# A decoder layer on one core: opening bias table written from 128 partitions, and splits, evacuations and side copies re-ordered

## The chip, the core and the metric

The kernel runs on one core of a Trainium2 chip. The metric is the device time of one execution in microseconds (us); lower is better. Names of engines: PE is TensorE (PEld its weight loads), DVE VectorE, ACT ScalarE, POOL GpSimd, SP the engine that only issues DMAs here.

## The reference

One post-norm decoder layer is applied to a prompt of 512 tokens and to 8 short sequences of 8 new tokens (576 token columns in all), width 1024, in float32:

```python
h = x @ w_in                                   # u | v | q | k | v_att | gate_A | gate_B
y_A = gelu(u) * (tril(W_s[g]) @ LN(gelu(v)) + b_s[g])
y_B = sliding-window attention, 16 heads over 4 key/value heads, window 128,
      scores + rel_bias[bucket(distance)], softmax with one learned sink per head
m   = (sigmoid(gate_A) * (y_A @ w_pa) + sigmoid(gate_B) * (y_B @ w_pb)) @ w_o
x   = LN(alpha * x + m);  x = LN(alpha * x + (silu(x @ w_gate) * (x @ w_up)) @ w_down)
```

What matters here is the bias: for the prompt, a block of 128 queries by 128 keys of head h needs `rel_bias[bucket((q - k) mod 128), h]`, a matrix that is one row of 128 numbers turned by one place per query.

## The kernel before

**Splits.** Every float32 product is made of three products of fp32r pieces: `split` (lines 114 to 116) makes `hi` on ACT and `lo = raw - hi` on DVE. All weights lie in one DRAM tensor `wall`, cut into units of 128 x 1024 in the order of use. `fetch` (L125) loads units into three `raw` buffers from SP's queue, so unit i+3 can be loaded only when DVE has made `lo` of unit i. `convert(n)` splits the units up to n and fetches two ahead; `unit` hands out the next one.

**The opening** is in `projections_and_attention`. Units 0 and 1 hold the first key tile (`ps0_0`) and the first query tile (`ps0_1`), worked through in eight steps k, each with its slice of x. After k = 1 `bias_products(0)` multiplies a selector matrix by the bias table into `bias_0` (16 heads x 512), DVE copies it into `bout` (L437), and `bias_tables` writes it to DRAM (`circ`, 1 MB: 16 heads, each of their rows repeated 128 times, L444), to read it back skewed as `Bsel` (two loads, L448). After k = 4 `bias_products(1)` does the rest for the sample. Then come `evac_k` (tiles `kt`, L469 and L472) and `evac_q` (tiles `qs` and `Z`, L484 to L495), the copies `XS` (L740, L741), the query tile `psq` of unit 2, and `values` (unit 3 and 4 into five `psav` banks, with the first two `attention_scores`, `sc`, between them).

**Attention** runs over 16 blocks (g, n). In each, `attention_turn` transposes the block's probabilities (`pT`), splits them (`pt`), and for n > 0 masks them on POOL by four selects (L600: `pc`, `pt`); `attention_values` multiplies (`po`) and adds the halves into `yB` (L616); the scores of the block two ahead follow; and a fill, `column_tile`, computes 128 more columns of `h` from one weight unit and evacuates them at once. `sample_keys`, called in block (3, 0), loads the cached keys and values and puts the new keys in by 16 small POOL copies (`kc`, L633). `gmlp` later needs `wd`, eight tiny DMAs (L841) and a select on POOL (L843).

A scheduler of the framework orders the instructions of each engine by its own costs, within the dependencies, except where `issue_after` or `manual_schedule` pins them. Each engine then runs its list in order; all DMAs named here stand in SP's queue.

Of the kernel before, what the change touches and what calls it, by code (L numbers as in the profile page):

```python
# [11 lines left out]
F32 = mybir.dt.float32  # L12
F32R = mybir.dt.float32r
I32 = mybir.dt.int32
AF = mybir.ActivationFunctionType
# [15 lines left out]
DS = 8  # L31
W = 128
# [7 lines left out]
NBIAS = W + DS * SK  # L40
# [37 lines left out]
class Builder:  # L78
# [337 lines left out]
    def bias_lookup(self):  # L416

        nc = self.nc
        n1 = NBKT + 1
        self.rb = rb = self.pk.tile([P, H], F32, name="rb")  # L420
        self.bout = []
        self.sel = sel = [self.C([w], F32, f"bsel{w}") for w in (512, NBIAS - 512)]
        nc.gpsimd.memset(rb[:n1], 1.0)
        nc.sync.dma_start(out=rb[:NBKT], in_=self.I["rel_bias"])
        nc.sync.dma_start(out=sel[0][:n1], in_=self.I["bias_sel"][:, :512])

    def bias_products(self, part):
        nc = self.nc
        n1 = NBKT + 1
        sel = self.sel[part]  # L430
        w = sel.shape[1]
        out = self.C([w], F32, f"bout{part}")
        self.bout.append(out)
        for c in range(0, w, 512):
            o = self.bank(f"bias{part}_{c}")[:H, : min(512, w - c)]
            self.mm(o, self.rb[:n1], sel[:n1, c : min(c + 512, w)], True, True)
            nc.vector.tensor_copy(out=out[:H, c : min(c + 512, w)], in_=o)  # L437

    def bias_tables(self):

        nc = self.nc
        cd = self.pd.tile([H, W, W], F32, name="circ")
        out0 = self.bout[0]
        nc.sync.dma_start(out=cd, in_=out0[:H, :W].unsqueeze(1).to_broadcast([H, W, W]))  # L444
        self.Bsel = [self.C([8, P], F32, f"Bsel{i}") for i in range(2)]
        for i in range(2):
            src = bass.AP(cd.tensor, cd.offset + 8 * i * W * W, [[W - 1, P], [W * W, 8], [1, P]])
            nc.sync.dma_start(out=self.Bsel[i][:], in_=src)  # L448

    def sample_bias(self):  # L450
        nc = self.nc
        sd = self.pd.tile([H, DS * SK], F32, name="samp")
        out0, out1 = self.bout
        self.bias_s = self.misc[:, 768:904]
        nc.sync.dma_start(out=sd[:, : 512 - W], in_=out0[:H, W:])
        nc.sync.dma_start(out=sd[:, 512 - W :], in_=out1[:H])
        nc.sync.dma_start(out=self.bias_s, in_=sd.rearrange("h (t j) -> (h t) j", t=DS))

# [17 lines left out]
    def evac_q(self, ps, c):  # L476
        nc = self.nc
        t = self.C([2, NT], F32R, f"qs{c}")
        self.qs[c] = t
        f = lambda a: a.rearrange("p (b c) -> p b c", b=2)  # L480
        for i in range(2):
            s = slice(64 * i, 64 * i + 64)
            o = slice(64 - 64 * i, 128 - 64 * i)
            nc.scalar.activation(out=f(t[s, i]), in_=ps[s, :, :HB], func=AF.Copy, scale=HD ** -0.5)  # L484
            nc.vector.scalar_tensor_tensor(
                out=f(t[o, i]), in0=ps[s, :, :HB], scalar=HD ** -0.5, in1=f(t[s, i]).bitcast(F32),
                op0=ALU.mult, op1=ALU.subtract)
            g, r = c // 2, 2 * (c % 2) + i
            src = ps[s, 1, HB - NS : HB].rearrange("p (a b t) -> p a b t", a=2, b=4)
            for a in range(2):  # L490
                dst = self.Z[64 * a : 64 * a + 64, g].rearrange("p b (r t) -> p b r t", r=4)[:, :, r]
                if a == i:
                    nc.scalar.activation(out=dst, in_=src[:, a], func=AF.Copy, scale=HD ** -0.5)
                else:
                    nc.vector.tensor_scalar_mul(dst, src[:, a], HD ** -0.5)  # L495

    def values(self, between):

        nc = self.nc
        u = [self.unit(4) for _ in range(2)]  # L500
        self.av = [self.C([2, G, 2 * HD], F32R, f"av{i}") for i in range(2)]
        vout = self.SG("vout")
        self.avS = self.misc[:, 512:768]
        for t in range(NB + 1):
            if t in (2, 4):
                between()
            o = self.bank(f"psav{t}")[:, :256]
# [77 lines left out]
    def attention_turn(self, g, n, pr):  # L585

        nc = self.nc
        po = self.bank(f"pT{g}_{n}")
        for r in range(4):
            self.last_turned = nc.tensor.transpose(  # L590
                po[:, P * r : P * r + P], pr[:, r], self.ident[:])
        pt = self.R([2, 512], F32R, f"pt{g}_{n}")
        self.split(pt[:, 0], pt[:, 1], po)
        if n == 0:
            return [(pt, 0)]
        pc = self.R([2, 512], F32R, f"pc{g}_{n}")
        f = lambda a: a.rearrange("p (h q) -> p h q", h=4)
        for out, sign, cmp in ((pc, 1, ALU.is_ge), (pt, -1, ALU.is_gt)):
            for i in range(2):
                nc.gpsimd.affine_select(  # L600
                    out=f(out[:, i]), in_=f(pt[:, i].bitcast(F32)), pattern=[[0, 4], [sign, P]],
                    compare_op=cmp, fill=0.0, base=0, channel_multiplier=-sign)
        return [(pc, n), (pt, n - 1)]
# [16 lines left out]
    def sample_keys(self):  # L620
        nc = self.nc
        f32c = lambda s, n: self.C(s, F32, n)
        kc = [f32c([2, G, SK], f"kc{i}") for i in range(2)]
        vc = [f32c([4, G * HD], f"vc{i}") for i in range(2)]
        for i in range(2):
            nc.sync.dma_start(out=kc[i][:, :, :, :W], in_=self.I["kcT"][:, 2 * i : 2 * i + 2])
            nc.sync.dma_start(out=vc[i][:], in_=self.I["vcT"][:, 4 * i : 4 * i + 4])
        for g in range(G):
            src = self.kraw[64 * (g % 2) : 64 * (g % 2) + 64, g // 2, P:]
            src = src.rearrange("p (a j b t) -> p a j b t", a=2, j=2, b=2)  # L630
# [76 lines left out]
    def projections_and_attention(self):  # L707
# [12 lines left out]
        for k in range(KC):  # L720
# [4 lines left out]
            for c in range(2):  # L725
                wh, wl = (w[:, k % 4, P * c : P * c + P] for w in u)
                for b in range(2):
# [2 lines left out]
                    self.mm(o, wh, xh[:, s], k == 0, False)  # L730
                    self.mm(o, wh, xl[:, s], False, False)
                    self.mm(o, wl, xh[:, s], False, k == KC - 1)
            if k == 1:
                self.bias_products(0)
                self.bias_tables()
            if k == 4:
                self.bias_products(1)
        self.evac_k(tiles[0], 0)
        self.evac_q(tiles[1], 0)
        nc.vector.tensor_copy(out=self.XS[:, :, :NS], in_=self.X[:, :, NP:NT].bitcast(F32))  # L740
        nc.vector.tensor_copy(out=self.XS[:, :, NS:], in_=self.X[:, :, NT + NP :].bitcast(F32))  # L741
        self.run(self.column_tile("q", 1))
        self.yB = []
        blocks = [(g, n) for g in range(G) for n in range(NB)]
        fills = FILLS
# [4 lines left out]
        for i, (g, n) in enumerate(blocks):  # L750
# [3 lines left out]
            if i:  # L754
                with self.tc.issue_after(self.last_turned.ins):
                    self.attention_values(*waiting)
            if i + 2 < len(blocks):
                probs.append(self.attention_scores(*blocks[i + 2]))
                if i + 4 == len(blocks):
                    kc, vc = self.sample_keys()  # L760
            elif i + 1 < len(blocks):
                S = self.sample_scores(kc)
            waiting = g, n, turned
# [2 lines left out]
            if i + 1 == len(blocks):  # L766
                with self.tc.issue_after(self.last_mm.ins):
                    self.attention_values(*waiting)
            self.run(fill)
        self.sample = S, vc  # L770

    def sample_first(self):
# [8 lines left out]
    def column_tile(self, kind, c):  # L781
# [3 lines left out]
        self.fm(ps, u, self.xact, ks=range(7))  # L785
        yield
        self.fm(ps, u, self.xact, ks=range(7, KC))
        if kind == "k":
            self.evac_k(ps, c)
        elif kind == "q":  # L790
# [34 lines left out]
    def gmlp(self):  # L825
# [12 lines left out]
        wd = self.pk.tile([P, 8, NS], F32, name="wd")  # L838
        nc.gpsimd.memset(wd[:NS], 0.0)
        for b in range(DB):  # L840
            nc.sync.dma_start(  # L841
                out=wd[DS * b : DS * b + DS, :, DS * b : DS * b + DS], in_=self.I["wsT"][:DS, :, :DS])
        nc.gpsimd.affine_select(  # L843
            out=wd[:NS], in_=wd[:NS], pattern=[[0, 8], [1, NS]], compare_op=ALU.is_ge, fill=0.0, base=0,
            channel_multiplier=-1)
# [602 lines left out]
```

## Time and profile before

| | before |
|---|---|
| median of 3 runs (lowest to highest) | 900.64 us (899.96 to 900.70) |
| the profiled execution: its time, its span | 901.71 us, 900.0 us |
| PE busy | 880.3 us, 98% of the span |
| DVE, ACT, POOL busy | 632.2, 403.5, 190.9 us |
| DMA | 91.98 MB, mean 102 GB/s |
| chain that ended last | PE 81%, DVE 9%, ACT 4%, DMA 3% |

The page gives busy times over the span. Idle PE time is what can be won, and it is found by the places where PE waits, with the clock that TensorE was granted there. A row of the timeline reads: start, duration, engine, line, operation, output and inputs, count, and in brackets the engine's idle time ahead of it with what ended it.

### The profile page before, as it was taken

The numbers are of one execution on the slowest core, as the hardware profiler recorded it, in microseconds if no ns is written. First come the engines' busy times: TensorE is split into PE (matmuls) and PEld (weight loads), VectorE is DVE, ScalarE is ACT, GpSimd is POOL, SyncE is SP. The second block draws the span as 40 slices with busy tenths as digits, with TensorE's granted clock in tenths as the row PEclk, the third lists the DMA queues.
The fourth block names the chain that finished last, engine by engine and source line by source line (L and its number), as shares of the span: only waits on it lengthen the run. The fifth ranks groups of instructions, "written<-read, shape, count | busy, mean of one in ns | idle before, by whom it ended". The sixth has DMA issues, their size and how long they took to land.

```text
span 900.0 us, 14730 instructions
## 1 busy us (share of the span) xinstructions
PE 880.3 (98%) x5915; PEld 824.0 (92%) x5915; DVE 632.2 (70%) x933; ACT 403.5 (45%) x767; POOL 190.9 (21%) x206
## 2 busy tenths in 40 slices
PE   9799999999999999999999999999999999999996
PEld 7699999997899999999988999999999998888885
DVE  4578978764789878957868777777777779224236
ACT  4456655666355437333442454444444457111110
POOL 2002223332333211233311312222222220000004
PEclk9899999999999999999999999999999999999999
DMA  7731212526223124223570023322233335322202
GB/s 213 211 104 47 71 49 59 169 82 203 87 71 103 60 94 173 87 86 118 188 240 29 1 71 94 94 95 94 94 94 95 94 94 188 90 75 94 71 4 102
DMA packets 32524, 91.98 MB, mean 102 GB/s; under 512 B 3974, under 2 KB 11030, under 8 KB 32424
## 3 DMA queue, kind: packets, MB, share of 16 engines
q1 hardware_dynamic: 32264, 88.86, 30.7%
q10 hardware_dynamic: 192, 2.18, 0.6%
q8 instruction: 46, 0.75, 0.3%
q14 instruction: 22, 0.18, 0.1%
HBM read 86.90 MB, written 6.10 MB: 103 GB/s over the span
## 4 chain that ended last, share of the span: by engine, by line
PE 81%; DVE 9%; ACT 4%; DMA 3%; issue 1%; POOL 1%; SPq 0%; POOLq 0%; ACTq 0%
PE d L296 16%; PE xf L296 14%; PE zf L296 7%; PE acc_v L296 6%; PE pspa L296 6%; PE acc_o L296 6%; PE xg L296 5%; PE yf L296 4%; DMA raw<-in_wall_dram 3%; PE ffn L296 3%; PE zg L296 2%; PE xp L296 2%; ACT work L576 2%; PE psg L296 1%; PE psu L296 1%
## 5 line engine op out<-in xcount | busy, mean ns | idle before, releaser
L116 DVE TENSOR_TENSOR lo<-raw,hi 128x1024 fp32r<-128x1024 f32 (+1 forms) x78 | 90.6, 1169 | 108.0 <-ACT hi L115 107.0
L116 DVE TENSOR_TENSOR glo<-raw,ghi 128x1024 fp32r<-128x1024 f32 (+1 forms) x93 | 100.8, 1087 | 55.2 <-ACT ghi L115 55.2
L115 ACT CAST hi<-raw 128x1024 fp32r<-128x1024 f32 (+1 forms) x78 | 75.6, 983 | 117.8 <-PE d L296 82.6
L296 PE MATMUL d<-hi,h 128*128 128x512 f32 (+1 forms) x440 | 128.0, 368 | 0.0
L115 ACT CAST ghi<-raw 128x1024 fp32r<-128x1024 f32 (+1 forms) x93 | 83.3, 899 | 58.7 <-DVE raw L178 54.1
L296 PEld LDWEIGHTS d<-hi,h 128*128 128x128 f32 x440 | 79.8, 188 | 13.8
L296 PE MATMUL d<-lo,h 128*128 128x512 f32 (+1 forms) x242 | 89.6, 370 | 0.0
L178 POOL TENSOR_TENSOR raw<-raw,t 128x512 f32<-128x512 f32 x31 | 40.7, 1314 | 197.9 <-DVE glo L116 151.4
L178 POOL TENSOR_TENSOR t<-raw,raw 128x512 f32<-128x512 f32 x31 | 43.1, 1389 | 116.3 <-DVE raw L178 116.3
L296 PE MATMUL xf<-x1T,ghi 128*128 128x288 f32 x320 | 65.0, 295 | 0.0
L116 DVE TENSOR_TENSOR glo<-t,ghi 128x1024 fp32r<-128x1024 f32 x31 | 64.5, 2082 | 0.0
L296 PEld LDWEIGHTS d<-lo,h 128*128 128x128 f32 x242 | 45.6, 189 | 7.8
L296 PEld LDWEIGHTS xf<-x1T,ghi 128*128 128x128 f32 x320 | 51.4, 188 | 0.2 <-DVE u L227 0.2
L326 POOL TENSOR_SCALAR lnr<-lnmv 128x1 f32<-128x1 f32 (+1 forms) x15 | 13.6, 904 | 169.2 <-DVE lnmv L344 165.9
L296 PE MATMUL xf<-x1T,glo 128*128 128x288 f32 x160 | 47.1, 294 | 0.0
L296 PE MATMUL acc_o<-hi,m 128*128 128x512 f32 x144 | 46.3, 391 | 0.0
L296 PE MATMUL pspa<-yA,hi 128*128 128x288 f32 x256 | 44.7, 295 | 0.3 <-DVE yA L116 0.3
L296 PE MATMUL psu<-X,hi 128*128 128x288 f32 x256 | 44.1, 294 | 0.0
L576 ACT ACTIVATE work<-work,att 128x128 f32<-128x128 f32 x64 | 25.0, 391 | 37.6 <-DVE att L573 37.6
L296 PE MATMUL acc_v<-hi,X 128*128 128x512 f32 x128 | 41.6, 391 | 0.0
L600 POOL TENSOR_SCALAR_AFFINE_SELECT pc<-pt 128x512 fp32r<-128x512 f32 x24 | 16.1, 672 | 112.7 <-ACT pt L115 108.4
L296 PE MATMUL psq<-X,hi 128*128 128x288 f32 x224 | 38.6, 294 | 0.0
(366 smaller groups left out, 2487.3 us busy)
## 6 DMA issues: line engine op xcount, KB each, us to landing
raw<-in_wall_dram SPq DMA_DIRECT2D x133, 512.0 KB
xr<-in_xT_dram SPq DMA_DIRECT2D x8, 288.0 KB
z<-in_xtok_dram SPq DMA_DIRECT2D x4, 512.0 KB
xraw<-in_xT_dram SPq DMA_DIRECT2D x3, 576.0 KB
out_y_prompt_dram<-z SPq DMA_DIRECT2D x3, 512.0 KB
circ<-bout SPq DMA_DIRECT2D x1, 1024.0 KB
Bsel<-circ SPq DMA_DIRECT2D x2, 512.0 KB
kc<-in_kcT_dram SPq DMA_DIRECT2D x2, 512.0 KB
```

Of the source, the lines that this page charges most:

```text
L115: self.nc.scalar.copy(out=hi, in_=src)
L116: return self.nc.vector.tensor_tensor(out=lo, in0=src, in1=hi.bitcast(F32), op=ALU.subtract)
L178: sub = lambda e, out, x, y: e.tensor_tensor(out=out, in0=x, in1=y, op=ALU.subtract)
L296: self.last_mm = self.nc.tensor.matmul(out, l, r, start=start, stop=stop, **more)
L326: self.nc.gpsimd.tensor_scalar_add(r[:n], mv[:n, 1:2], EPS)
L576: nc.scalar.activation(out=pr[:, r], in_=sel[:, r], func=AF.Exp, bias=nm[:, r : r + 1], accum_out=rs[:, r : r + 1])
L600: nc.gpsimd.affine_select(out=f(out[:, i]), in_=f(pt[:, i].bitcast(F32)), pattern=[[0, 4], [sign, P]], compare_op=cmp, fill=0.0, base=0, c ...
```

## The change

It does five things. The bias row is computed for 128 partitions (each head eight times, by a repeated copy `rb8` made on POOL), repeated four times along the free axis by DVE, and written to `circ` as 512 pieces of 512 numbers instead of 2048 pieces of 128. `circ` and `Bsel` stand behind the splits of unit 2, and so behind the loads of units 3 and 4. The splits of units 3 and 4 stand ahead of the first evacuations, those of units 5 and 6 behind them (`first_read`). The `XS` copies stand behind `evac_q` of the second query tile. In attention, the evacuation of a q or k fill stands behind the next block's `pT` and `po`; the cached loads and the `kc` copies stand behind the last select made so far, and the `wd` loads behind the cached values.

```diff
@@ bias_lookup @@
+        first = self.C([512 + P], F32, "bsel0")
+        self.rb8 = first[:, 512:]
...
+        nc.gpsimd.tensor_copy(
+            out=self.rb8[:n1].rearrange("p (h m) -> p h m", m=8), in_=rb[:n1].unsqueeze(2).to_broadcast([n1, H, 8]))
@@ bias_products @@
+        if part == 0:
+            o = self.bank("bias0")
+            self.mm(o[:, :W], self.rb8[:n1], sel[:n1, :W], True, True)
+            self.mm(o[:H, W:], self.rb[:n1], sel[:n1, W:], True, True)
+            self.circ = out[:, :512].rearrange("p (r i) -> p r i", r=4)
+            nc.vector.tensor_copy(out=self.circ, in_=o[:, :W].unsqueeze(1).to_broadcast([P, 4, W]))
+            nc.vector.tensor_copy(out=out[:H, 512:], in_=o[:H, W:])
...
@@ bias_tables @@
-        nc.sync.dma_start(out=cd, in_=out0[:H, :W].unsqueeze(1).to_broadcast([H, W, W]))
+        nc.sync.dma_start(
+            out=cd.rearrange("h (m a r) i -> (h m) a r i", m=8, a=4),
+            in_=self.circ.unsqueeze(1).to_broadcast([P, 4, 4, W]))
@@ values @@
-        u = [self.unit(4) for _ in range(2)]
+        u = []
+        for _ in range(2):
+            with self.tc.issue_after(self.first_read.ins):
+                u.append(self.unit(4))
@@ projections_and_attention @@
-            if k == 1:
-                self.bias_products(0)
-                self.bias_tables()
-            if k == 4:
-                self.bias_products(1)
+            if k in (1, 4):
+                self.bias_products(k // 4)
+        self.convert(2)
+        self.bias_tables()
+        self.convert(4)
         self.evac_k(tiles[0], 0)
         self.evac_q(tiles[1], 0)
-        nc.vector.tensor_copy(out=self.XS[:, :, :NS], in_=self.X[:, :, NP:NT].bitcast(F32))
-        nc.vector.tensor_copy(out=self.XS[:, :, NS:], in_=self.X[:, :, NT + NP :].bitcast(F32))
+        self.first_read = self.evacuated
         self.run(self.column_tile("q", 1))
+        with self.tc.issue_after(self.placed.ins):
+            nc.vector.tensor_copy(out=self.XS[:, :, :NS], in_=self.X[:, :, NP:NT].bitcast(F32))
+            nc.vector.tensor_copy(out=self.XS[:, :, NS:], in_=self.X[:, :, NT + NP :].bitcast(F32))
...
                     self.attention_values(*waiting)
+                self.run(fill)
...
                 if i + 4 == len(blocks):
-                    kc, vc = self.sample_keys()
+                    with self.tc.issue_after(self.selected.ins):
+                        kc, vc = self.sample_keys()
...
-            self.run(fill)
+            next(fill, None)
+            if fills[i][0] not in "qk":
+                self.run(fill)
+        self.run(fill)
@@ column_tile @@
         self.fm(ps, u, self.xact, ks=range(7, KC))
+        yield
@@ gmlp @@
-            nc.sync.dma_start(
-                out=wd[DS * b : DS * b + DS, :, DS * b : DS * b + DS], in_=self.I["wsT"][:DS, :, :DS])
+            with self.tc.issue_after(self.loaded.ins):
+                nc.sync.dma_start(
+                    out=wd[DS * b : DS * b + DS, :, DS * b : DS * b + DS], in_=self.I["wsT"][:DS, :, :DS])
```

How the instructions move shows at three places. On SP, in the opening (`raw_229` and `raw_327` are the loads of units 3 and 4 before, `raw_226` and `raw_301` in the changed kernel; `misc` is the last small table). Before:

```order
L813 DMA misc<-in_sinks_p_dram 128x1
L444 DMA circ<-bout_191 2048x1x128
L125 DMA raw_229<-in_wall_dram 128x1024
L125 DMA raw_327<-in_wall_dram 128x1024
L448 DMA Bsel_197<-circ 128x8x128
L448 DMA Bsel_198<-circ 128x8x128
L125 DMA raw_333<-in_wall_dram 128x1024
```

In the changed kernel:

```order
L839 DMA misc<-in_sinks_p_dram 128x1
L125 DMA raw_226<-in_wall_dram 128x1024
L125 DMA raw_301<-in_wall_dram 128x1024
L457 DMA circ<-bout_192 512x1x512
L125 DMA raw_313<-in_wall_dram 128x1024
L125 DMA raw_319<-in_wall_dram 128x1024
L463 DMA Bsel_309<-circ 128x8x128
L463 DMA Bsel_310<-circ 128x8x128
```

The loads of units 3 and 4 went ahead of the write of `circ`, and those of units 5 and 6 ahead of its reading back.

On DVE, from the last split of unit 2 on (`lo_336` and `lo_399` are the splits of units 3 and 4 before, `lo_316` and `lo_322` in the changed kernel). Before:

```order
L116 TENSOR_TENSOR lo_330<-raw_138,hi_329 128x1024
L116 TENSOR_TENSOR lo_336<-raw_229,hi_335 128x1024
L437 COPY bout_255<-bias_0_256 16x512
L437 COPY bout_255<-bias_512_259 16x192
L116 TENSOR_TENSOR lo_399<-raw_327,hi_398 128x1024
L472 TENSOR_TENSOR kt_304<-ps_0_151,kt_304 64x576 x2
L472 TENSOR_TENSOR kt_305<-ps_0_151,kt_305 64x576 x2
L485 SCALAR_TENSOR_TENSOR qs_315<-ps_1_152,qs_315 64x576
L116 TENSOR_TENSOR lo_405<-raw_333,hi_404 128x1024
L495 TENSOR_SCALAR Z<-ps_1_152 64x4x8
L740 CAST XS<-X 128x8x64
L741 CAST XS<-X 128x8x64
```

In the changed kernel:

```order
L116 TENSOR_TENSOR lo_304<-raw_139,hi_303 128x1024
L450 COPY bout_252<-bias_0_253 16x512
L450 COPY bout_252<-bias_512_256 16x192
L116 TENSOR_TENSOR lo_316<-raw_226,hi_315 128x1024
L116 TENSOR_TENSOR lo_322<-raw_301,hi_321 128x1024
L487 TENSOR_TENSOR kt_325<-ps_0_152,kt_325 64x576 x2
L487 TENSOR_TENSOR kt_326<-ps_0_152,kt_326 64x576 x2
L500 SCALAR_TENSOR_TENSOR qs_336<-ps_1_153,qs_336 64x576
L510 TENSOR_SCALAR Z<-ps_1_153 64x4x8
L500 SCALAR_TENSOR_TENSOR qs_394<-psq_345,qs_394 64x576
```

The bank copies `bout` went ahead of the split of unit 3; the split of unit 5 and the `XS` copies left the evacuations.

On POOL, around block (2, 3) (`pt_3` and `pc_3` belong to it, `pc_1` to block (3, 1)). Before:

```order
L600 AFFINE_SELECT pt_2_1726<-pt_2_1726 128x512 x2
L633 COPY kc_1971<-misc 64x2x8 x8
L600 AFFINE_SELECT pc_3_1833<-pt_3_1830 128x512
L633 COPY kc_1972<-misc 64x2x8 x8
L600 AFFINE_SELECT pc_3_1833<-pt_3_1830 128x512
L600 AFFINE_SELECT pt_3_1830<-pt_3_1830 128x512 x2
L600 AFFINE_SELECT pc_1_2060<-pt_1_2057 128x512 x2
```

In the changed kernel (the two `kc` rows alternate, eight of each):

```order
L618 AFFINE_SELECT pt_2_1729<-pt_2_1729 128x512 x2
L618 AFFINE_SELECT pc_3_1836<-pt_3_1833 128x512 x2
L618 AFFINE_SELECT pt_3_1833<-pt_3_1833 128x512 x2
L651 COPY kc_1974<-misc 64x2x8
L651 COPY kc_1975<-misc 64x2x8
...
L870 AFFINE_SELECT wd<-wd 64x512
L618 AFFINE_SELECT pc_1_2063<-pt_1_2060 128x512 x2
```

The copies left the middle of block (2, 3)'s selects and stand behind them, and the `wd` select, which came far earlier, now stands ahead of block (3, 1)'s.

## Rows read from the trace of the kernel before

**Rows 1.** The page, part 1: busy us, share of the span, instructions.

```profile
PE 880.3 (98%) x5915; PEld 824.0 (92%) x5915; DVE 632.2 (70%) x933; ACT 403.5 (45%) x767; POOL 190.9 (21%) x206
```

**Rows 2.** PE's timeline in the opening: bias product, last query matmul, the two waits.

```profile
7.96 1.03 PE L296 MATMUL bias<-bsel,rb 33*16 33x512 f32 x2
...
27.45 0.43 PE L296 MATMUL psq<-X,lo 128*128 128x288 f32 x2
31.93 0.36 PE L296 MATMUL psav<-hi,X 128*128 128x256 f32 x1 [4.04 <-DVE bout L437]
...
42.16 1.12 PE L296 MATMUL sc<-kt,qs 128*128 128x256 f32 x6 [2.53 <-DVE qs L485]
```

**Rows 3.** Windows: A:B length, PE, PEld, DVE, ACT, POOL busy, clock, DMA share, GB/s.

```profile
15.50:26.00 10.50, 10.50 (x74) 9.35 (x73) 0.91 (x1) 0.00 (x0) 0.99 (x1) 1.00 0.73 94
...
31.93:36.12 4.19, 4.19 (x22) 4.19 (x23) 2.83 (x5) 2.14 (x5) 0.00 (x0) 0.59 1.07 383
...
42.16:46.29 4.13, 4.13 (x21) 4.13 (x22) 3.40 (x8) 1.03 (x3) 0.08 (x1) 0.59 0.21 53
46.29:50.48 4.19, 4.19 (x38) 4.19 (x37) 2.48 (x6) 1.33 (x6) 0.58 (x1) 1.00 0.40 127
53.00:200.00 147.00, 144.51 (x1117) 139.40 (x1116) 116.75 (x222) 87.96 (x253) 38.47 (x67) 1.00 0.27 84
...
26.30:27.60 1.30, 1.30 (x13) 1.30 (x11) 0.00 (x0) 0.00 (x0) 0.00 (x0) 1.00 1.02 382
```

**Rows 4.** SP's timeline in the opening: when each DMA is issued, and how long that takes.

```profile
13.91 0.71 SPq L444 DMA_DIRECT2D circ<-bout  x1
14.72 8.00 SPq L125 DMA_DIRECT2D raw<-in_wall_dram  x2
...
40.45 4.29 SPq L841 DMA_DIRECT2D wd<-in_wsT_dram  x6
```

**Rows 5.** Timelines of ACT (first row) and DVE (the others) in the opening.

```profile
28.89 1.04 ACT L115 CAST hi<-raw 128x1024 fp32r<-128x1024 f32 x1 [13.74 <-DMA raw<-in_wall_dram]
...
13.22 0.67 DVE L437 COPY bout<-bias 16x512 f32<-16x512 f32 x1
...
29.96 1.23 DVE L116 TENSOR_TENSOR lo<-raw,hi 128x1024 fp32r<-128x1024 f32 x1 [13.56 <-ACT hi L115]
31.11 0.94 DVE L437 COPY bout<-bias 16x512 f32<-16x512 f32 x2
...
40.57 0.75 DVE L485 SCALAR_TENSOR_TENSOR qs<-psq,qs 64x576 fp32r<-64x576 f32 x1
```

**Rows 6.** PE's waits over the span: us in total, times, longest.

```profile
PE po L296 <- DVE yB L616: 1.0, 1, 1.0
PE po L296 <- POOL pc L600: 0.8, 1, 0.8
```

**Rows 7.** DVE's timeline in attention: two blocks' evacuations, one operation at two speeds.

```profile
127.08 0.76 DVE L485 SCALAR_TENSOR_TENSOR qs<-psq,qs 64x576 fp32r<-64x576 f32 x1
...
127.98 0.85 DVE L616 TENSOR_TENSOR yB<-po,bot 64x256 f32<-64x256 f32 x2
...
164.93 0.61 DVE L573 TENSOR_TENSOR att<-att,misc 128x4 f32<-128x4 f32 x1
...
173.22 0.16 DVE L573 TENSOR_TENSOR att<-att,misc 128x4 f32<-128x4 f32 x1
```

**Rows 8.** POOL's timeline: the wd select, the kc copies, block (3, 1)'s first select.

```profile
46.21 0.66 POOL L843 TENSOR_SCALAR_AFFINE_SELECT wd<-wd 64x512 f32<-64x512 f32 x1 [29.71 <-DMA wd<-in_wsT_dram]
...
155.69 2.29 POOL L633 COPY kc<-misc 64x16 f32<-64x16 f32 x8
...
161.86 2.38 POOL L633 COPY kc<-misc 64x16 f32<-64x16 f32 x8
...
177.18 0.75 POOL L600 TENSOR_SCALAR_AFFINE_SELECT pc<-pt 128x512 fp32r<-128x512 f32 x1 [11.06 <-ACT pt L115]
```

**Rows 9.** SP's timeline in attention: the weight load that will stand between the wd loads.

```profile
169.62 0.33 SPq L125 DMA_DIRECT2D raw<-in_wall_dram  x1
```

More of the change, by code (lines that the diff above doesn't have):

```diff
@@ L421, in bias_lookup @@
         self.bout = []
-        self.sel = sel = [self.C([w], F32, f"bsel{w}") for w in (512, NBIAS - 512)]
+        first = self.C([512 + P], F32, "bsel0")
+        self.rb8 = first[:, 512:]
+        self.sel = sel = [first[:, :512], self.C([NBIAS - 512], F32, "bsel1")]
         nc.gpsimd.memset(rb[:n1], 1.0)
@@ L431, in bias_products @@
         w = sel.shape[1]
-        out = self.C([w], F32, f"bout{part}")
+        out = self.C([w if part else 2 * 512 - W], F32, f"bout{part}")
+        if part == 0:
[5 more added lines that the diff above has]
+            nc.vector.tensor_copy(out=out[:H, 512:], in_=o[:H, W:])
+            self.bout.append(out[:, 512:])
+            return
         self.bout.append(out)
@@ L442, in bias_tables @@
         cd = self.pd.tile([H, W, W], F32, name="circ")
-        out0 = self.bout[0]
-        nc.sync.dma_start(out=cd, in_=out0[:H, :W].unsqueeze(1).to_broadcast([H, W, W]))
+        nc.sync.dma_start(
+            out=cd.rearrange("h (m a r) i -> (h m) a r i", m=8, a=4),
+            in_=self.circ.unsqueeze(1).to_broadcast([P, 4, 4, W]))
         self.Bsel = [self.C([8, P], F32, f"Bsel{i}") for i in range(2)]
@@ L454, in sample_bias @@
         self.bias_s = self.misc[:, 768:904]
-        nc.sync.dma_start(out=sd[:, : 512 - W], in_=out0[:H, W:])
+        nc.sync.dma_start(out=sd[:, : 512 - W], in_=out0[:H])
         nc.sync.dma_start(out=sd[:, 512 - W :], in_=out1[:H])
@@ L492, in evac_q @@
                 if a == i:
-                    nc.scalar.activation(out=dst, in_=src[:, a], func=AF.Copy, scale=HD ** -0.5)
+                    self.evacuated = nc.scalar.activation(out=dst, in_=src[:, a], func=AF.Copy, scale=HD ** -0.5)
                 else:
-                    nc.vector.tensor_scalar_mul(dst, src[:, a], HD ** -0.5)
+                    self.placed = nc.vector.tensor_scalar_mul(dst, src[:, a], HD ** -0.5)
     def values(self, between):
         nc = self.nc
-        u = [self.unit(4) for _ in range(2)]
+        u = []
+        for _ in range(2):
+            with self.tc.issue_after(self.first_read.ins):
+                u.append(self.unit(4))
         self.av = [self.C([2, G, 2 * HD], F32R, f"av{i}") for i in range(2)]
@@ L599, in attention_turn @@
             for i in range(2):
-                nc.gpsimd.affine_select(
+                self.selected = nc.gpsimd.affine_select(
                     out=f(out[:, i]), in_=f(pt[:, i].bitcast(F32)), pattern=[[0, 4], [sign, P]],
@@ L626, in sample_keys @@
             nc.sync.dma_start(out=kc[i][:, :, :, :W], in_=self.I["kcT"][:, 2 * i : 2 * i + 2])
-            nc.sync.dma_start(out=vc[i][:], in_=self.I["vcT"][:, 4 * i : 4 * i + 4])
+            self.loaded = nc.sync.dma_start(out=vc[i][:], in_=self.I["vcT"][:, 4 * i : 4 * i + 4])
         for g in range(G):
```

## Prediction

> **What bounds the kernel now.** I read the page first: PE is busy for 880.3 of 900.0 us [rows 1], so only some 20 us of idle time can be won, and a change that moves no matmul work can win only there and in time at a lower clock. PE's timeline says where: after the last matmul of the first lone query tile it stands idle for 4.04 us and resumes at 31.93; at its first scores it stands for 2.53 us more and resumes at 42.16 [rows 2]. The windows add what follows each wait: the stretch after the first has a mean granted clock of 0.59 for 4.19 us, the one after the second 0.59 for 4.13 us, and the next is back at 1.00 [rows 3]. TensorE has two levels, 1.2 and 2.4 GHz, so most of both stretches ran at the lower, behind idle PE; from 53 to 200 us the clock is 1.00 throughout [rows 3].
>
> Then the cause. The page's releaser for the first wait is a DVE copy of a bias bank, but that is the last of a chain: the copy stands at 31.11 behind the `lo` of unit 3 at 29.96, which waited 13.56 us for ACT's `hi`, which waited 13.74 us for a weight load until 28.89 [rows 5]. SP's timeline shows the load queued behind the 1 MB write of `circ`, issued at 13.91, with two loads behind it that took 8.00 us to issue [rows 4]. During that write the DMAs moved 94 GB/s, against 382 once loads run again [rows 3]. So late weights held up DVE, and DVE and ACT then had splits, bank copies and evacuations to do at once; the second wait ends on the last of these evacuations.
>
> **The change, part by part.**
>
> *Loads of units 3 and 4 ahead of `circ`.* Both need free `raw` buffers. Unit 3 goes as soon as the tables are issued, and unit 4 when unit 1 is split; both splits lie before the bank copy at 13.22 [rows 5]. Two units at 382 GB/s are 2.7 us for 1.05 MB, so even if they begin only when `circ` was issued, at 13.91 [rows 4], they land by 16.7 us. DVE's list then holds the last x slices, `lo` of unit 2, two bank copies (0.94 together) and `lo` of units 3 and 4 (1.23 each) [rows 5]. Before, DVE had finished unit 2 when the 13.56 us wait for ACT began, at 29.96 - 13.56 = 16.4 us. The added bank copy below and these three items make it 16.4 + 0.7 + 0.9 + 2.5 = 20.5 us; the banks of the second product come late enough to add about 1. That is 21.5 us, and PE wants unit 3 at 27.9 us (the end of the query tile in rows 2). The first wait goes with 6 us to spare: 4.04 us. With it goes the slow clock behind it, 4.19 x (1 - 0.59) = 1.72 us.
>
> *Evacuations with nothing in between.* With units 3 and 4 split, the key tile and half of the first query tile are evacuated while PE works on `psq`. What is left at 27.9 us is, on ACT, three query halves and one `hi`, and on DVE three query halves of 0.75 [rows 2, 5], one `lo` of 1.23, and some `Z` rows. Taken as one chain with ACT's halves at 0.75 as well: first half 0.75 + 0.75, second half 0.75, `Z` and the wait for it 0.5, `hi` 1.04 and `lo` 1.23 beside ACT's last half, last half 0.75: 5.8 us, ending at 33.7. PE first has 48 `psav` matmuls; 38 take 4.19 us at full clock [rows 3], so 48 take 5.3 us, to 33.2. The last half is wanted only by the last 4 of 16 score matmuls, 1.3 us later, at 34.5. I take the second wait as gone, 2.53 us, and its slow clock, 4.13 x 0.41 = 1.69 us. The margin is only 0.8 us; if the chain is longer, the wait comes back in part, which is a rival below.
>
> *Opening sum:* 4.04 + 1.72 + 2.53 + 1.69 = 9.98 us won.
>
> *The bias row for 128 partitions.* One product becomes two, of the same 512 columns: the old one took 1.03 us [rows 2]; I take 0.1 us more for a second start, between 0 and 1.03. It stands ten matmuls later; 38 took 4.19 us [rows 3], so 0.11 each, and it is due 1.1 us after the old 7.96, near 9.1. The POOL copy `rb8` ahead of it has no row of its own: it lies between a `kc` copy (2.29 / 8 = 0.29 us) and a select of 0.75 [rows 8], and the table it copies was there when the old product ran, at 7.96 [rows 2], so it ends by 8.7 us: nothing. On DVE one copy of 0.67 [rows 5] becomes two, one of the same 512 numbers over more partitions and one of 384, so 0.5 to 0.75 us more, ahead of the last x slices. DVE was done with these and unit 2 at 16.4, so now by 17.2; PE has 72 matmuls from these slices to 27.9, 0.12 us each for 288 columns, and reaches them near 19: nothing.
>
> *`circ` itself.* Its price falls on nobody, if units 5 and 6, now behind it, land by about 30 us. At the old 94 GB/s it takes 1.05 / 94 = 11.2 us from some 15 us on, to 26; a load behind it lands by 27.5, `Bsel` by 31, and scores reach the table only after 34. At 382 GB/s it would be 2.7 us. Both ends give the same sum.
>
> *Attention.* PE waits 1.0 us once for `yB`, and 0.8 us once for `pc` [rows 6]. The first is DVE's list: a query half of 0.76 at 127.08 and `Z` stood ahead of `yB` at 127.98 [rows 7]; now that half stands behind `yB`, which comes 0.9 us earlier. The second is eight `kc` copies of 2.38 us between the two `pc` selects [rows 8]; now all stand behind the block's selects. I take both as gone: 1.8 us, between 0 and the 147.00 - 144.51 = 2.49 us that PE idles there in all [rows 3].
>
> *What the moved steps are put in front of.* The `wd` select on POOL waits for eight `wd` DMAs, the last three behind the weight load issued at 169.62 [rows 9]. Six such DMAs took 4.29 us to issue [rows 4], so three take 2.1 us, and the old select began 46.21 - 44.74 = 1.5 us after the last one: 169.9 + 2.1 + 1.5 = 173.5, plus 0.66 for itself, is 174.2, on the old time scale. Block (3, 1)'s first select is due at 177.18 [rows 8]: 3 us to spare, so nothing. Without that cover POOL would hold block (3, 1)'s selects, and PE behind them. Sixteen `kc` copies (4.7 us) end before it. On SP the three `wd` issues delay a weight load by 2.1 us; three buffers of such loads cover it.
>
> **Sum.** 9.98 + 1.8 - 0.1 = 11.7 us. The profiled execution took 901.71 us, so the same would take 890.0; the median of the runs shown is 1.07 us lower, which gives **889.0 us**.
>
> **The rivals.**
>
> *A. As forecast,* 887.3 to 891.0 (the attention gain from 2.5 down to 0.8, with 1.0 either way for the measurement and the smaller sizes): 0.66.
>
> *B. Attention gives its gain back.* POOL and DVE hold each other up: DVE's tiny `att` step at 164.93 took 0.61 us beside POOL's selects, and 0.16 at 173.22 without [rows 7]. The `kc` copies now come in one piece beside block (3, 0)'s softmax, and late query halves stand beside the next block's scores. A wait of 1 to 3 us then takes the place of those removed: 900.64 - 9.98 + 0.1 = 890.8, and up to 892. Against it: DVE's work per block is the same, and the copies lie in a block with idle time. 0.15. The Trainium skill (SBUF — State Buffer, Who interferes with whom) says that a DVE instruction with two SBUF inputs and a POOL instruction that reads SBUF exclude each other for the whole instruction. The trace agrees in the 0.61 against 0.16.
>
> *C. The second wait comes back.* The chain of 5.8 us needs to be only 0.8 us longer for PE to stand before its last scores. Then up to 2.53 + 1.69 us are kept: 889.0 + 4.2 = 893.2. For it: these evacuations pass between ACT and DVE, each waiting for the other. 0.13.
>
> *D. Nothing happens,* as the loads of units 3 and 4 still wait, for buffers or in the queue, until the write is done: about 900.6. The order on SP speaks against it. 0.03.
>
> *E. Slower: the write of `circ` becomes the wait.* Unit 5's `hi` stands on ACT ahead of the last query half, and its load now stands behind `circ`. If the write from 128 partitions, each piece read four times, is slow, PE stands before the last four scores with a slow clock (1.69) behind it. To end over 902.4 the loss must be 13.4 us, so a stall of 11.7 us, to 46.2; back through a half, `lo` and `hi` (3.0) and a load (1.4), `circ` would end at 41.8: 27 us for 1.05 MB, 39 GB/s. Nothing in the trace moves large pieces at less than 94. 0.03.
>
> **How the numbers follow.** A and B together hold 0.81 and reach from 887.3 to 892, so the range is 887.3 to 892.2. About 0.2% (1.8 us) is what a measurement of this kernel can tell from no change: A, B and C are faster by more (0.94), D is the same (0.03), E slower (0.03).
>
> **What would show it.** In the new profile PE should have no wait of over 0.5 us between 21 and 50 us and a granted clock of 1.00 there; the first `psav` at about 27.8 and the first scores near 33; `hi` of units 3 and 4 before 18 us; `circ` issued behind two loads. In attention the waits for `yB` (1.0) and `pc` (0.8) should be missing. A wait on `qs` before `sc` shows C, one on `pc` or `po` B, one on ACT's `hi` near 34 us E. A time outside 887 to 893 makes the prediction wrong, and so does a gain that is not in the first 55 us.

## The result and the profile after

| | before | changed |
|---|---|---|
| median of 4 runs, one comparison (lowest to highest) | 900.67 us (899.96 to 901.38) | 891.39 us (891.19 to 891.56) |
| ratio, 95% interval | | 0.9897 (0.988 to 0.9914) |
| the profiled execution: its time, its span | 901.71, 900.0 us | 891.56, 889.8 us |
| first `psq` matmul, first `pT` | 21.40, 59.45 us | 21.77, 49.77 us |
| `pT` of the last block | 191.23 us | 180.73 us |
| last matmul | 891.36 us | 881.19 us |

The kernel is 9.3 us (1.0%) faster. That lies in the range of 887.3 to 892.2, but 2.4 us above the 889.0 forecast, above the 891.0 at which forecast A ends, and within rival B's 890.8 to 892. Ratios, here and below, are to the kernel before, run beside the other; brackets hold the 95% interval. The last three lines of the table say in which part of the program the gain arises: 9.68 us up to the first `pT`, 10.50 up to the last one, 10.17 at the last matmul.

The page of the changed kernel, part 1, answers to [rows 1]:

```profile
PE 875.9 (98%) x5917; PEld 821.2 (92%) x5917; DVE 631.7 (71%) x934; ACT 404.5 (45%) x767; POOL 192.2 (22%) x207
```

PE's timeline of the changed kernel in the opening (the two bias products, the end of the query tile, the first `psav`, all 16 score matmuls); it answers to [rows 2], and neither wait is left:

```profile
9.45 0.49 PE L296 MATMUL bias<-bsel 33*128 33x128 f32 x2
9.86 0.81 PE L296 MATMUL bias<-bsel,rb 33*16 33x384 f32 x2
...
27.82 0.43 PE L296 MATMUL psq<-X,lo 128*128 128x288 f32 x2
28.09 0.28 PE L296 MATMUL psav<-hi,X 128*128 128x256 f32 x1
...
33.84 2.08 PE L296 MATMUL sc<-kt,qs 128*128 128x256 f32 x16
```

The windows, with columns as in [rows 3]: the stretch of the write and the loads, and the whole opening from the first `psq` to the first `pT`. PE is busy for all of its 28.00 us, at full clock:

```profile
14.00:20.00 6.00, 6.00 (x40) 4.84 (x39) 4.00 (x6) 2.73 (x3) 1.82 (x2) 1.00 1.02 388
...
21.77:49.77 28.00, 28.00 (x227) 28.00 (x226) 20.11 (x39) 15.65 (x43) 0.00 (x0) 1.00 0.44 127
```

The timelines of SP, ACT and DVE answer to [rows 4, 5]. `circ` is issued behind two loads, and `hi` of units 3 and 4 begins at 16.22 and 17.56, where unit 3's began at 28.89. DVE has split both by 21.58, and evacuates the last query half by 33.96:

```profile
8.00 3.87 SPq L125 DMA_DIRECT2D raw<-in_wall_dram  x2
13.48 0.64 SPq L457 DMA_DIRECT2D circ<-bout  x1
16.41 4.40 SPq L125 DMA_DIRECT2D raw<-in_wall_dram  x2
...
16.22 1.05 ACT L115 CAST hi<-raw 128x1024 fp32r<-128x1024 f32 x1 [1.58 <-DMA raw<-in_wall_dram]
17.56 1.04 ACT L115 CAST hi<-raw 128x1024 fp32r<-128x1024 f32 x1 [0.29 <-DMA raw<-in_wall_dram]
...
19.25 2.33 DVE L116 TENSOR_TENSOR lo<-raw,hi 128x1024 fp32r<-128x1024 f32 x2
...
33.20 0.76 DVE L500 SCALAR_TENSOR_TENSOR qs<-psq,qs 64x576 fp32r<-64x576 f32 x1
```

In attention the waits for `yB` and `pc` of [rows 6] are missing, and three others stand in PE's timeline instead:

```profile
95.36 0.80 PE L296 MATMUL psu<-X,hi 128*128 128x288 f32 x4 [1.33 <-ACT Z L508]
...
130.16 0.80 PE L296 MATMUL psu<-X,hi 128*128 128x288 f32 x4 [0.44 <-ACT Z L508]
...
174.30 0.80 PE L296 MATMUL psg<-X,hi 128*128 128x288 f32 x4 [1.02 <-ACT u L822]
```

**What the idle column leaves out.** A matmul's end is modelled, so a wait inside a short series shows only in part. PE's rows of the kernel before, at the `pc` wait of block (3, 0):

```profile
163.76 0.47 PE L296 MATMUL po<-pc,av 128*128 128x512 f32 x1
165.00 0.50 PE L296 MATMUL po<-pc,av 128*128 128x512 f32 x1 [0.76 <-POOL pc L600]
165.58 1.09 PE L296 MATMUL po<-pt,av 128*128 128x512 f32 x2
166.51 1.12 PE L296 MATMUL sc<-kt,qs 128*128 128x256 f32 x8
```

From the first `po` to `sc` it takes 2.75 us. Without a wait the same four matmuls of the changed kernel take 1.01 (154.16 to 155.17):

```profile
154.16 0.71 PE L296 MATMUL po<-pc,av 128*128 128x512 f32 x2
...
155.17 1.10 PE L296 MATMUL sc<-kt,qs 128*128 128x256 f32 x8
```

So the wait costs 1.74 us and not 0.76. I therefore count by blocks, from the first `pT` of one to that of the next. An undisturbed block takes 8.64 us (7.73 in block 0, 8.18 behind a block n = 0, 9.13 in block 14 with the sample's scores, as in experiment 9); the table gives what blocks take above that. Blocks are numbered 0 to 15, so that block 12 is (3, 0).

| kernel | block: excess in us | first to last `pT` |
|---|---|---|
| before | 5: 0.39, 6: 0.20, 8: 1.28 (`yB`), 11: 0.65 (`pt`), 12: 1.75 (`pc`), 14: 0.11 | 131.78 |
| changed | 4: 0.41, 5: 1.60 (`Z`), 9: 0.62 (`Z`), 14: 0.97 (`u`) | 130.96 |

The change took 3.68 us out of blocks 8, 11 and 12 and put 3.19 into blocks 5, 9 and 14, with 0.41 in block 4. The 0.20 of block 6 went too, and the 0.39 of block 5 is inside its 1.60 or gone. Net gain: 131.78 - 130.96 = 0.82 us. These blocks make up 0.67 of it; the rest is the 0.11 of before in block 14, and 0.04 in block 10.

### The profile page after: what moved, and what is told of

Same layout as the page of the kernel before. It is cut to its first block, busy times and chain, and to the rows that moved or that the text cites. A ratio compares the mean times of both kernels' runs of the same rounds, so it can differ in the third digit from the quotient of the medians.

```text
span 889.8 us, 14740 instructions
## 1 busy us (share of the span) xinstructions
PE 875.9 (98%) x5917; PEld 821.2 (92%) x5917; DVE 631.7 (71%) x934; ACT 404.5 (45%) x767; POOL 192.2 (22%) x207
## 4 chain that ended last, share of the span: by engine, by line
PE 83%; DVE 10%; ACT 4%; issue 2%; DMA 1%; POOL 0%; POOLq 0%; ACTq 0%
PE d L296 16%; PE xf L296 14%; PE zf L296 7%; PE acc_o L296 6%; PE pspa L296 6%; PE xg L296 5%; PE acc_v L296 5%; PE yf L296 4%; PE ffn L296 3%; PE zg L296 3%; PE xp L296 2%; ACT work L594 2%; DVE lo L116 2%; PE psq L296 2%; PE psav L296 2%
## 5 line engine op out<-in xcount | busy, mean ns | idle before, releaser
L296 PEld LDWEIGHTS psu<-X,hi 128*128 128x128 f32 x256 | 37.1, 188 | 2.2 <-ACT Z L508 2.2
```

The source lines that it names most:

```text
L296: self.last_mm = self.nc.tensor.matmul(out, l, r, start=start, stop=stop, **more)
```

## Experiments

**Theory 1**: each new wait comes from one place in an order. The later evacuation of q4 and q7 holds a PSUM tile that a later fill wants, and u7's copy stands late on ACT. **Theory 2**: DVE and ACT run almost a block behind PE, whatever the order. When PE comes earlier, it waits somewhere else for as long.

DVE's rows and ACT's last `Z` row for the evacuation of q4, in the kernel before (the block's `pT` is at 92.64) and in the changed kernel (`pT` at 82.96):

```profile
98.71 0.75 DVE L485 SCALAR_TENSOR_TENSOR qs<-psq,qs 64x576 fp32r<-64x576 f32 x1
99.50 0.69 DVE L116 TENSOR_TENSOR pt<-pT,pt 128x512 fp32r<-128x512 f32 x1
...
101.32 0.76 DVE L485 SCALAR_TENSOR_TENSOR qs<-psq,qs 64x576 fp32r<-64x576 f32 x1
...
102.22 0.19 ACT L493 ACTIVATE Z<-psq 64x32 f32<-64x32 f32 x1 [1.13 <-DVE Z L495]
```

```profile
89.64 0.69 DVE L116 TENSOR_TENSOR pt<-pT,pt 128x512 fp32r<-128x512 f32 x1
90.25 0.84 DVE L634 TENSOR_TENSOR yB<-po,bot 64x256 f32<-64x256 f32 x2
91.01 0.74 DVE L500 SCALAR_TENSOR_TENSOR qs<-psq,qs 64x576 fp32r<-64x576 f32 x1
...
94.22 0.76 DVE L500 SCALAR_TENSOR_TENSOR qs<-psq,qs 64x576 fp32r<-64x576 f32 x1
...
95.12 0.19 ACT L508 ACTIVATE Z<-psq 64x32 f32<-64x32 f32 x1 [0.62 <-DVE Z L510]
```

DVE splits `pt` 6.7 to 6.9 us behind `pT` in both, so its lag did not change. But the evacuation ends 12.3 us behind `pT` instead of 9.8, and the fill that waits for its tile could have begun at 94.03. In block 4, too, the fill begins only when a late evacuation ends, that of k1 on ACT: at 85.46, 0.05 us behind it.

**1. The evacuations back, the rest changed.**

```diff
-                self.run(fill)
...
+            self.run(fill)
@@ column_tile @@
-        yield
```

> The changed kernel with one part undone: a q or k fill is evacuated at once, as before, and not behind the next block's pT and po. The waits of the changed kernel in attention are 1.33 us (95.36) and 0.44 us (130.16) for the release of a query fill's bank, and 1.02 us (174.30) for a u copy. Theory 1 (the later place of the evacuation holds the bank: it ends 12.3 us after the block's pT, where it ended 9.6 us after it before): the 1.33 and 0.44 go, the yB wait of 1.0 comes back, the 1.02 stays; PE idle after the first pT falls from 2.85 to about 2.1 us, time 890.6. Theory 2 (DVE and ACT run almost a block behind PE, and PE's arrival sets the wait, in whatever order they evacuate): waits of about the same sum, 2.5 to 2.9 us, at other places, time 891.4.

Ratio 0.9898 (0.9882 to 0.9915). The excesses are those of before in blocks 5, 6, 8 and 11 (0.39, 0.20, 1.27, 0.66), none in 4 and 12, and 1.49 in block 14. First to last `pT`: 131.38. So theory 1 is right on `Z` and `yB`: the two `Z` waits go and the `yB` wait returns. The last wait grew where I expected it to stay, so the sum is no better: PE idles 3.1 us in the 150.55 us from the first `pT`, where theory 1 had 2.1 and theory 2 up to 2.9. In its sum the run came out nearer to theory 2.

**2. Attention alone, with the opening of before.** The core of the diff against the kernel before:

```diff
+                self.run(fill)
...
+                    with self.tc.issue_after(self.selected.ins):
+                        kc, vc = self.sample_keys()
...
+            next(fill, None)
+            if fills[i][0] not in "qk":
+                self.run(fill)
```

> The kernel before with the attention part of the change alone (late q and k evacuation, cached keys and kc copies behind the selects, wd loads behind the cached values). By the prediction's sum it wins 1.8 us: 898.9. Theory 1: the late evacuation makes its own waits here too, about 1.8 us, and the yB, pc and pt waits of 2.5 us in all go: 900.0 to 901, PE idle after the first pT 1.8 to 2.9 us. Theory 2: PE idles 2.5 us there as before, 900.6.

Ratio 0.9989 (0.998 to 0.9998), a gain of about 1.0 us (0.2 to 1.8), where the prediction's sum had 1.8. Its blocks take 131.09 us in all, 0.7 less than before, with the same three excesses as the changed kernel (1.73, 0.70, 1.00). The new waits thus need no changed opening. More interesting is its opening, whose order is that of before but for the `wd` loads, which have left it: 36.38 us from the first `psq` to the first `pT` in this execution, 38.05 in the other. I return to this below.

**3. The opening alone, with the attention of before.**

```diff
-                    with self.tc.issue_after(self.selected.ins):
-                        kc, vc = self.sample_keys()
+                    kc, vc = self.sample_keys()
...
-            with self.tc.issue_after(self.loaded.ins):
```

with the edit of experiment 1.

> The changed kernel with the whole attention part undone, so that the opening alone is changed. First pT at 49.8 us as in the changed kernel by every theory. By the prediction's sum the opening alone is worth 9.9 us less the 0.3 us by which the first query tile began later: 891.1, and the attention part would have added 1.8 us. Theory 1: the waits are those of before (yB 1.0, pc 0.8, pt 0.4), PE idle after the first pT 2.5 us, time 891.0, so 0.3 us under the changed kernel. Theory 2: idle 2.5 to 2.9 us, not the same places, 891.0 to 891.4.

Ratio 0.9897 (0.9882 to 0.9912): the whole gain, within the interval. Excesses as before (1.27, 0.64, 1.73), first to last `pT` 131.48. The attention part is thus worth 131.48 - 130.96 = 0.5 us. Theory 1 had the waits right, but not that this run would be 0.3 us faster than the changed kernel.

With experiments 1 and 3 the wait of block 14 can be read. They differ only in the `kc` and `wd` moves. ACT's copy of u7 and PE's first `psg` matmul, in the kernel before, then in experiment 3, then in experiment 1:

```profile
184.00 0.63 ACT L796 COPY u<-psu 128x576 f32<-128x576 f32 x1
...
184.68 0.80 PE L296 MATMUL psg<-X,hi 128*128 128x288 f32 x4
```

```profile
174.50 0.63 ACT L816 COPY u<-psu 128x576 f32<-128x576 f32 x1
...
175.19 0.80 PE L296 MATMUL psg<-X,hi 128*128 128x288 f32 x4
```

```profile
174.18 0.63 ACT L817 COPY u<-psu 128x576 f32<-128x576 f32 x1
...
174.86 0.80 PE L296 MATMUL psg<-X,hi 128*128 128x288 f32 x4 [1.52 <-ACT u L817]
```

The sample's scores take both other large tiles, so `psg` needs the tile of u7 itself. In the kernel before, its copy ended at 184.63 and `psg` began at 184.68: hardly a wait, but no margin either, since the same 0.05 us pass in experiment 1, where PE does wait for the copy (174.81 to 174.86). The `kc` and `wd` moves, which end the `pc` wait, brought PE there 1.85 us earlier (1.52 + 175.19 - 174.86), the copy only 0.32 us earlier. So the limit was there before the change, hidden behind the `pc` wait.

**4. Fills in another order.**

```diff
-"q3 u0 k1 q4 q5 u1 q6 q7 u2 u3 u4 u5 u6 u7 g0 g1"
+"q3 k1 q4 u0 q5 u1 q6 u2 q7 u3 u4 u5 u6 u7 g0 g1"
```

> The changed kernel with the fills in another order (q3 k1 q4 u0 q5 u1 q6 u2 q7 u3 in place of q3 u0 k1 q4 q5 u1 q6 q7 u2 u3), so that two query fills, each with some 1.9 us of DVE work against none for a u fill, never follow each other after the first three; the work is the same. Theory 1: a wait of 0.4 to 1.3 us stands wherever a fill takes the bank of a query fill two blocks earlier, so about as many waits, 2.5 to 3.5 us in all, 891.4 to 892. Theory 2 (what counts is how far DVE has fallen behind): three evacuations in a row at the start make a longer wait there (2 us or more, before block 4), and none later: PE idle 2 to 4 us, 891 to 892.5, but the 0.44 us of block 9 is gone.

Ratio 0.9906 (0.9891 to 0.9921). First to last `pT` 130.89, with excesses of 0.97, 0.81, 0.84 and 0.95 in blocks 3, 8, 10 and 14, and a further wait of 1.56 us for a `g` copy behind the last block. The waits follow the evacuations about and make much the same sum: block 9's went, as theory 2 had it, but its wait of 2 us or more ahead of block 4 did not come. This run doesn't tell the theories apart.

**5. The order of the opening alone, `circ` written from 16 partitions as before.** The bias functions are those of before; the order of calls stays changed.

```diff
-            out=cd.rearrange("h (m a r) i -> (h m) a r i", m=8, a=4),
-            in_=self.circ.unsqueeze(1).to_broadcast([P, 4, 4, W]))
+        nc.sync.dma_start(out=cd, in_=out0[:H, :W].unsqueeze(1).to_broadcast([H, W, W]))
```

> The changed kernel, but the bias row is made for 16 partitions and written to circ in 2048 pieces of 128 numbers, as before; the order of loads, splits and evacuations stays changed. The prediction's account (the loads of units 3 and 4 must only stand ahead of the write; even at 94 GB/s the write is over by 26 us and unit 5 lands by 27.5): no PE wait over 0.5 us between 21 and 50 us, first pT at 49.5 us (0.3 us less than in the changed kernel, as one bias product is gone), 891. Rival (the fast write is the gain): the write of 11 us holds unit 5 and Bsel, PE waits 2 us or more before its last scores, with up to 1.7 us of slow clock behind it, 893 to 895.

Ratio 0.9886 (0.9869 to 0.9902); 28.00 us from the first `psq` to the first `pT` with no wait, as in the changed kernel. SP's rows show how slow the old write is: `Bsel`, which waits for it, is issued at 27.41 and not at 20.90, and nobody needs it earlier.

```profile
14.03 0.71 SPq L444 DMA_DIRECT2D circ<-bout  x1
16.68 7.26 SPq L125 DMA_DIRECT2D raw<-in_wall_dram  x2
27.41 1.01 SPq L448 DMA_DIRECT2D Bsel<-circ  x2
```

**6. The write alone, from 128 partitions, in the order of before.**

```diff
-            if k in (1, 4):
-                self.bias_products(k // 4)
-        self.convert(2)
-        self.bias_tables()
-        self.convert(4)
+            if k == 1:
+                self.bias_products(0)
+                self.bias_tables()
+            if k == 4:
+                self.bias_products(1)
```

and `XS` and the units of `values` without `issue_after`.

> The changed kernel with the order of loads, splits, evacuations and XS copies in the opening as before; circ is written from 128 partitions, ahead of the loads of units 3 and 4. If the write takes some 5 us and not 11 to 15 us, these loads land by about 20 us. The prediction's account (the order was the cause, through late loads): the first wait is gone or under 1 us here too, as the loads are in time by either way; the second, of evacuations mixed with splits, may stay in part: 891 to 894. Rival (the order of the loads is needed): the waits of 4.04 and 2.53 us stay for the most part, 897 to 900.

Ratio 0.9903 (0.9888 to 0.9917). The first wait is gone, and of the second 0.62 us is left; 28.95 us from `psq` to `pT`. So the first wait has two cures, a load ahead of the write or a fast write, and either is enough.

**7. The splits and evacuations in the old order, loads and write changed.** As the diff above, but with `convert(2)` and `bias_tables()` kept where the change has them.

> The changed kernel with the splits of units 3 to 6 and the XS copies where they were before (no set order against the evacuations); circ stands behind the loads of units 3 and 4 and is written from 128 partitions. The prediction's account: the first wait is gone, the second (evacuations mixed with splits, 2.53 us and 1.69 us of slow clock) comes back in part, 893 to 896. Rival (the second wait was only a result of the late loads): no wait over 0.5 us, 891 to 892.

Ratio 0.9909 (0.9895 to 0.9924). PE's one wait in this opening:

```profile
35.75 0.98 PE L296 MATMUL sc<-kt,qs 128*128 128x256 f32 x6 [1.26 <-DVE qs L500]
```

The windows ahead of that wait and behind it; the clock is 1.00 in both:

```profile
30.00:34.40 4.40, 4.40 (x38) 4.29 (x36) 4.14 (x8) 2.96 (x6) 0.00 (x0) 1.00 0.46 146
35.75:40.00 4.25, 4.25 (x35) 4.24 (x36) 3.45 (x9) 1.08 (x4) 0.00 (x0) 1.00 0.02 6
```

29.59 us from `psq` to `pT`. With the loads in time, the set order is worth 1.59 us of opening (0.95 by experiment 6). About half of the second wait or more was thus a result of the late loads.

**8. Two moves more on the changed kernel**: only q6 is evacuated late, and u7's copy stands ahead of the last block's exponentials on ACT (`between` runs u7's fill).

```diff
-            if fills[i][0] not in "qk":
+            if fills[i] != ("q", 6):
                 self.run(fill)
@@ attention_scores, `between` given for block (3, 3) alone @@
+        if between is not None:
+            between()
+        with ExitStack() as pinned:
+            if between is not None:
+                pinned.enter_context(self.tc.issue_after(self.copied_u.ins))
...
```

> The changed kernel with two moves more: only the sixth query fill is evacuated late, all others at once; and in block (3, 1) the copy of u7 stands on ACT ahead of block (3, 3)'s exponentials and not behind them. Theory 1 (each of these waits is one place in an order: q4's and q7's late evacuation make 1.33 and 0.44, q6's early one makes the yB wait of 1.0, u7's late copy makes 1.02 to 1.52): all of them go, 0.4 us is left (pt), PE idle after the first pT 0.3 to 0.6 us against 2.85, time about 2.4 us under the changed kernel: 889. Theory 2 (DVE and ACT set the pace, and PE only waits elsewhere when it comes earlier): 1.5 us or more of waits at new places, 890.5 to 891.5.

Ratio 0.9877 (0.9862 to 0.9891). Excesses of 0.38, 0.21, 0.13, 0.51 and 0.65 in blocks 5, 6, 9, 10 and 11; those of `yB`, `Z`, `pc` and `u` are all gone; first to last `pT` 129.12. The copy of u7 runs at 170.77 and `psg` begins at 172.47:

```profile
170.77 0.63 ACT L830 COPY u<-psu 128x576 f32<-128x576 f32 x1
...
172.47 0.79 PE L296 MATMUL psg<-X,hi 128*128 128x288 f32 x4
...
187.26 0.49 PE L296 MATMUL po<-pt,av 128*128 128x512 f32 x1 [0.60 <-POOL pt L623]
```

Theory 1 holds for the waits named. Theory 2 is right in a smaller way: waits for `pt` come back, one of 0.60 us at 187.26 and the new 0.51 of block 10. PE idles 1.22 us in the 150.55 from the first `pT`, between the 0.3 to 0.6 of theory 1 and the 1.5 of theory 2.

**9. The changed kernel, the two moves, and the two moves with the old write, side by side.**

> The changed kernel itself, beside the next two on one chip, so that differences of 1 us can be read. Every theory: ratio to the kernel before 0.9875 to 0.99, the same waits as in its first profile (1.33, 0.44, 1.02).

> The kernel with two moves more (only the sixth query fill evacuated late; the copy of u7 ahead of block (3, 3)'s exponentials), again, beside the changed kernel. Its first profile idled 1.22 us against 2.86 in 150.55 us from the first pT. Theory 1: 1.3 us less than the changed kernel (1.0 to 2.0). Theory 2: within 0.5 us of it.

> The same with the bias row made for 16 partitions and circ written as before the change, behind the loads of units 3 and 4. If the write from 128 partitions is worth nothing behind the loads: the same as the kernel with two moves, within 0.5 us. If it is worth something that the single run of the order alone (891.18) hid: 0.5 us or more above it, with PE waits before 50 us.

Medians 891.37 (891.20 to 891.82), 890.49 (889.96 to 890.63) and 889.89 us (889.82 to 890.15); ratios to before 0.9896 (0.988 to 0.9912), 0.9883 (0.9866 to 0.9901) and 0.9879 (0.9864 to 0.9895). The two moves win 0.9 us, less than theory 1's 1.0 to 2.0 and more than theory 2's 0.5. The old write costs nothing behind the loads. It is 0.6 us lower. In the profiles 0.3 of that lies ahead of the first `psq` (21.86 against 22.16), 0.2 behind the last `pT`, and I know a cause for neither. The simplest version is also the fastest here.

## Why the prediction was right, and where it was not

*Opening: right.* The sum of 9.98 us was for two waits and their slow clock. From the first `psq` to the first `pT` the profile gives 38.05 - 28.00 = 10.05. Each mark came about as stated: `psav` at 28.09 (27.8), scores at 33.84 (33), both `hi` begun before 18 us, `circ` behind two loads, no wait, clock 1.00. So did the steps between: `lo` of unit 4 was done at 21.58 (21.5), the last query half at 33.96 (33.7). Only unit 4 landed later than the 16.7 stated, near 17.5, which the spare time took up. That the sum agrees so closely owes something to luck: it was read from the same execution of before, and against the opening of experiment 2 the gain is 36.38 - 28.00 = 8.38. Two parts of the account are now sharper. The 128 partitions give nothing once the order is set (experiments 5 and 9), as the step on `circ` said. And the second wait was only partly a matter of order: 0.62 to 1.26 us of it stays when the loads are early by themselves (experiments 6 and 7).

*Bias row: too small to read.* I took 0.1 us; `psq` began 0.37 us later. But it began at 21.78 in experiment 2, whose opening has the old order and product. Over all profiles it begins at 21.40 to 21.86 with the old product and at 21.77 to 22.20 with the new, so some 0.2 us of the 0.37 may be the product and the rest is not.

*Attention: the step that failed.* It took two waits as gone, "1.8 us, between 0 and the 147.00 - 144.51 = 2.49 us that PE idles there in all". The waits did go, and were worth more than I took: 3.68 us with `pt`, by block periods. What failed is the other side of that step. I asked what the moved evacuation stands behind, but not who waits for the tile that it holds: 1.60 and 0.62 us, and 0.41 in block 4 (in experiment 1 all three go, and the 0.39 of before returns). And I did not look for what is late next behind the `pc` wait, where u7's copy had no margin: 0.97. Net 0.82 us instead of 1.8 against the profile, 0.7 in experiment 2, and 0.5 against experiment 3.

*Rival B: its time came, its main reason did not.* It said 890.8 to 892, with a wait of 1 to 3 us in place of those removed, because POOL and DVE hold each other. Of its two causes, the late query halves did make waits, but through the tile that they hold (experiment 1), and not at `pc` or `po`, where B looked for them. The other, the `kc` copies in one piece, made DVE faster there: the two `att` steps took 0.60 and 0.55 us beside `pt` selects (experiment 3, first three rows), and 0.20 each beside the `kc` copies (experiment 1, last two rows).

```profile
155.42 1.22 POOL L618 TENSOR_SCALAR_AFFINE_SELECT pt<-pt 128x512 fp32r<-128x512 f32 x2
155.46 0.60 DVE L591 TENSOR_TENSOR att<-att,misc 128x4 f32<-128x4 f32 x1
156.10 0.55 DVE L592 TENSOR_TENSOR att<-att,misc 128x4 f32<-128x4 f32 x1
...
154.18 3.39 POOL L651 COPY kc<-misc 64x16 f32<-64x16 f32 x16
155.53 0.20 DVE L591 TENSOR_TENSOR att<-att,misc 128x4 f32<-128x4 f32 x1
```

The Trainium skill (SBUF — State Buffer, Who interferes with whom) says that a DVE instruction with two SBUF inputs contends with a POOL instruction that reads SBUF, and that the one issued second waits until the other is done. The runs agree: the second `att` step ends at 156.65, with the second select (156.64). In 0.20 against 0.60 us they show that here short POOL copies (3.39 / 16 = 0.21 us each) held a DVE step for less than selects of 0.61. C, D and E did not come: no wait on `qs`, a gain in the first 50 us, and no wait on ACT's `hi`.

*The sum against the median.* Against its own execution the prediction said 890.0, and the changed kernel's took 891.56. But for rounding, the 1.56 us are attention (0.98), the start (0.27 beyond the 0.1), 0.33 lost between the last `pT` and the last matmul and 0.02 at the end, less 0.07 won in the opening. The other 0.83 us came with the median: I subtracted 1.07 us (1.0 with the rounding), since the profiled execution of before stood that far above it, but the changed kernel's stands only 0.17 above its own. The opening of before is what varied between two profiles, by 1.67 us, so part of that offset was probably in the waits that the change removed. The range was right although forecast A was not: it took in B's times, and ended 0.2 us above them without a term for that.

## What to carry to other kernels

When an evacuation is moved back, look up which product takes its PSUM tile next and how many us lie between; the wait that goes is worth only what the next-latest producer allows. Price a wait inside a short series by the period of the loop, not by the idle column. Where a slow DMA holds up loads in its queue, try their order first: here, once the loads stood ahead of the write, its speed no longer mattered.

## What the runs showed of the hardware

The opening of before took 38.05 us in one execution and, in experiment 2, 36.38. In the first, the stretch behind the 4.04 us wait had a mean clock of 0.59, PE then waited 2.53 us at the scores, and ran at 0.59 again [rows 3]. In the second, behind a wait of 3.81 us, PE came slower to the scores and waited only 1.48 us, and the clock stayed at 1.00:

```profile
32.08:36.30 4.22, 4.22 (x20) 4.22 (x21) 2.86 (x5) 2.17 (x5) 0.00 (x0) 0.50 1.07 381
36.30:40.40 4.10, 4.10 (x30) 4.10 (x30) 3.96 (x7) 3.64 (x7) 0.00 (x0) 0.81 0.17 66
...
42.31:46.40 4.09, 4.09 (x33) 4.08 (x34) 3.90 (x9) 1.03 (x3) 0.00 (x0) 1.00 0.17 55
```

DVE's list runs alike in both (the query half of [rows 5] at 40.57 runs at 40.71), and the scores wait for it: they begin 20.76 and 20.53 us behind the first `psq`. So the slow matmuls ahead of the scores only shortened the wait there, and of the 1.67 us by which the two differ, 1.44 lie behind it. Waits of 1.26 us (experiment 7) and 1.33 us (at 95.36 in the changed kernel) also left the clock at 1.00. So a wait cost its own length, or, at the longest wait at the scores, 1.7 times that (2.53 + 1.69). The runs of before spread over 1.4 us in the first comparison, those of the changed kernel, which has neither wait, over 0.4. Of the 26 runs of before under 903 us in the later comparisons, the 17 with a mean clock of 0.994 took 900.8 us on average, the nine with 0.991 to 0.993 took 901.8. These numbers fit the clock as a cause of part of the spread; it was not tested by itself.
